# Another order of block products, splits and DMA additions in the up projection of a hybrid transformer block

## The chip, the cores and the metric

The kernel runs on one core of a Trainium2 chip. Its engines work side by side and meet through semaphores: TensorE (PE, with its weight loads as PEld), VectorE (DVE), ScalarE (ACT), GpSimd (POOL) and SyncE (SP). SP issues plain DMA loads; POOL issues the DMAs that add what they read onto what lies in the on-chip buffer. The metric is the device time of one execution in microseconds. The time before is the median of three runs.

## The reference

One layer: a hybrid mixer, a cross attention and a convolutional feed-forward part, each followed by a layer norm. All is float32. The change is in the first half of the feed-forward part:

```python
def conv_ffn(x, w_up, conv_w, conv_b, w_down):
    u = causal_dwconv(x @ w_up, conv_w, conv_b)
    gate, val = jnp.split(u, 2, axis=-1)
    return (jax.nn.gelu(gate) * val) @ w_down
```

Here x is 512 tokens by 1024, w_up is 1024 by 5632 (gate and val have 2816 columns each), and w_down is 2816 by 1024.

## The kernel before

The kernel is one long program of stages; a scheduler places the instructions of each engine in a fixed order when the program is built. Each float32 product is made of three matmuls over a high and a low part: ACT casts the weights to the high part `wh` (line 125), DVE subtracts it to get the low part `wl` (line 126), and PE runs the three matmuls of lines 155 to 157. Four buffers each of `wh` and `wl` rotate, so the cast for a product can start when the product four places earlier is done.

The up projection is cut into 11 quads, q = 0 to 10. A quad takes 256 gate and 256 val columns of w_up, in four blocks B11, B12, B21 and B22 of 128 partitions by 1024 floats (512 KB; the first index is the half of the contraction, the second gate or val). Seven block products M1 to M7 instead of eight make a quad, in the manner of Strassen and Winograd. Each is 24 matmuls of 256 columns. On the side of the tokens the combinations are made once (`forms`, tiles `xf`). On the side of the weights they are made for each quad by DMA, in place:

- M1, M2 and M3 use B11, B21 and B22 as loaded.
- After M3's split, B12 is added onto B22. M7 uses that sum.
- After M1's split, the new B22 is added onto B11. M6 uses that sum.
- After M2's split, the new B11 is added onto B21. M4 uses that sum.
- M5 uses T1, a second copy of B11 onto which B12 is added.

So three additions follow one another, B22, then B11, then B21; this is the chain of weight sums. For q = 0 the sum of B22 is made in a slot of its own (T3) before the stage. The blocks lie in nine slots: halves of the three `raw` buffers, `rawx`, and the two halves of `hf[5]`. In the trace they show as `raw`, `rawx` and `hf`; an addition onto B11 in `raw` from B22 in `hf` is `raw<-hf`, and one that reads B12 from HBM is `raw<-in_ffn_w_up_dram`. A slot is given back when its last product has been split, and `take` hands out the slot that was given back longest ago. Loads stand in order in SP's queue and additions in POOL's; a waiting one holds up what stands behind it.

`seq` (lines 850 to 857) is the order of the products. From q = 3 on a group of seven is M1, M2, M7, M6 of q, M3 of q + 1, then M4, M5 of q. `step(i)` writes product i and, with it, the split of product i + 3, the additions which that split allows, and loads ahead of need (`AHEAD`, lines 994 to 1000). M1, M6 and M5 accumulate in one PSUM bank and M7 and M4 in another: between two of them ACT copies the bank out (`keep`, line 926), so M6 waits for the copy m1, M4 for m7 and M5 for u2. These copies, the splits and the convolution (lines 939 to 946) share ACT and DVE. In the shown rows of engine order `wh_...<-raw_...` is the split of a product, and `m1_`, `m3_`, `m7_`, `u2_` are the copies after M1, M3, M7 and M6.

Of the kernel before, what the change touches and what calls it, by code (L numbers as in the profile page):

```python
# [32 lines left out]
NQ = NPAIR // 2  # L33
# [7 lines left out]
def hybrid_block_kernel(  # L41
# [34 lines left out]
    def mm_bank():  # L76
        return pm.tile([P, 512], F32, name="mm", tag="mm", bufs=5)

    def mx_bank():
        return pm.tile([P, 512], F32, name="mx", tag="mx", bufs=3)  # L80
# [38 lines left out]
    def split(src, shape, skew=0):  # L119
        h = wp.tile([P, 1152], F32R, name="wh", tag="wh", bufs=4)[:, skew:skew + 1024]  # L120
        l = wp.tile([P, 1152], F32R, name="wl", tag="wl", bufs=4)[:, skew:skew + 1024]
        a, c = shape
        hv = h.rearrange("p (a c) -> p a c", a=a)
        lv = l.rearrange("p (a c) -> p a c", a=a)
        A.copy(hv, src)  # L125
        V.tensor_sub(lv, src, f32(hv))  # L126
        return hv, lv
# [141 lines left out]
    def tt(name):  # L269
        return q1p.tile([P, 512], F32, name=name, tag="T", bufs=20)  # L270
# [122 lines left out]
    for i, h, l in col_units(w_in0, HQ, 4):  # L393
        ps = mm_bank()
        col_tile(ps, h, l, feat(xTh), feat(xTl))
        q = tt("q")
# [438 lines left out]
    slots, free = [], list(range(9))  # L835

    def ffn_begin():
# [3 lines left out]
        for q in range(3):  # L841
# [5 lines left out]
    load, add = nc.sync.dma_start, lambda d, s_: nc.gpsimd.dma_start(d, s_, accum_op=OP.add)  # L847
    blk = lambda q, n: ffn_w_up[q, int(n[1]) - 1, int(n[2]) - 1]
    FORM = {"M1": "A11", "M2": "A12", "M3": "S4", "M4": "A22", "M5": "S1", "M6": "S2", "M7": "S3"}
    seq = [(n, q) for q in range(3) for n in ("M1", "M2")]  # L850
    seq += [(n, int(q)) for n, q in (w.split(".") for w in
            "M3.0 M7.0 M6.0 M3.1 M4.0 M5.0 M3.2 M7.1 M6.1 M3.3 M4.1 M5.1 M7.2 M6.2 M4.2 M5.2".split())]
    for q in range(3, NQ):
        if q + 1 < NQ:
            seq += [("M1", q), ("M2", q), ("M7", q), ("M6", q), ("M3", q + 1), ("M4", q), ("M5", q)]
        else:
            seq += [(n, q) for n in ("M1", "M7", "M2", "M6", "M4", "M5")]
    held, units = {}, {}

    def take(q, n):  # L860

        ok = [f for f in free if not (q >= NQ - 2 and 5 <= f < 7) and not (q >= 7 and f == 8)]
        held[q, n] = ok[0]
        free.remove(ok[0])
        return slots[ok[0]]

    at = lambda q, n: slots[held[q, n]]

    def drop(q, n):
        free.append(held.pop((q, n)))  # L870

    def loads(q, names):
        for n in names:
            load(take(q, n), blk(q, n if n != "T1" else "B11"))

    def first_t(q):
        loads(q, ["T1"])
        add(at(q, "T1"), blk(q, "B12"))

    def split_of(i):  # L880

        n, q = seq[i]
        src = {"M1": "B11", "M2": "B21", "M3": "B22", "M4": "B21", "M5": "T1", "M6": "B11", "M7": "B22"}[n]
        if n == "M7" and (q, "T3") in held:
            src = "T3"
        units[i] = split(at(q, src), (8, P), 16)
        t3 = "T3" if (q, "T3") in held else "B22"
        if n == "M1":
            if (q, t3) in held and (q, "summed") in units:
                add(at(q, "B11"), at(q, t3))  # L890
        if n == "M2":
            if (q, "summed") in units:
                add(at(q, "B21"), at(q, "B11"))
        if n == "M3":
            units[q, "summed"] = True
            if t3 == "B22":
                add(at(q, "B22"), blk(q, "B12"))
            else:
                drop(q, "B22")
            if q not in (1, 2):  # L900
                first_t(q)
            if q < 3:
                add(at(q, "B11"), at(q, t3))
                add(at(q, "B21"), at(q, "B11"))
        if n == "M7":
            drop(q, src)
        if n == "M6":
            drop(q, "B11")
        if n == "M5":
            drop(q, "T1")  # L910
        if n == "M4":
            drop(q, "B21")

    def product(bank, i, first, last):
        (h, l), (fh, fl) = units.pop(i), forms[FORM[seq[i][0]]]
        for j in range(2):
            for k in range(4):
                mm3(bank[:, j * 256:(j + 1) * 256], h[:, 4 * j + k, :], l[:, 4 * j + k, :], fh[:, k, :], fl[:, k, :],
                    first and j == 0 and k == 0, last and j == 1 and k == 3)
# [4 lines left out]
    def keep(q, name, bank):  # L924
        t = t2(name)
        A.copy(t, bank)  # L926
        kept[q, name] = g2(t)

    def put(q, c, half, bank, name):
        V.tensor_tensor(uus[q][:, c, :, half * 256:(half + 1) * 256], g2(bank), kept[q, name], op=OP.add)  # L930

    def conv_pieces(q):
        y = {}

        def taps(c, j):
            ft = j * NPAIR + 2 * q + c
            u, f = uus[q][:, c, j, :], t2("fc")
            w = lambda i: ncols[:, i * 44 + ft:i * 44 + ft + 1] if c else col(FCW + i * 44 + ft)
            A.activation(f, u, AF.Identity, bias=col(FCB + ft), scale=w(2))  # L939
            if j:  # L940
                A.activation(y[c, 0], y[c, 0], AF.Gelu_apprx_tanh)  # L941
            for d in (1, 2):
                V.scalar_tensor_tensor(f[:, d:], u[:, :S - d], w(2 - d), f[:, d:], op0=OP.mult, op1=OP.add)  # L943
            y[c, j] = f

        mul = lambda c: V.tensor_mul(hslice(2 * q + c), y[c, 0], y[c, 1])
        return [lambda: taps(1, 0), lambda: taps(1, 1), lambda: (mul(1), taps(0, 0)), lambda: taps(0, 1),
                lambda: mul(0)]

    def step(i):  # L950

        n, q = seq[i]
        if n == "M1":
            banks[q, "P"] = mm_bank()
            uus[q] = (hf[3 + q] if q < 2 else raws[q % 2]).rearrange("p (c j t) -> p c j t", c=2, j=2)
        if n == "M7":
            banks[q, "Q"] = mm_bank()
        if n in ("M2", "M3"):
            banks[q, n] = mx_bank()
        b = banks[q, {"M1": "P", "M6": "P", "M5": "P", "M7": "Q", "M4": "Q"}.get(n, n)]  # L960
        for f in posts:
            f()
        posts.clear()
        if i + 3 < len(seq):
            split_of(i + 3)
        elif i + 3 - len(seq) < len(down_first):
            down_first[i + 3 - len(seq)]()

        for m, names in AHEAD.get(i, ()):
            if names == "T1":  # L970
                first_t(m)
            else:
                loads(m, names)
        product(b, i, n in ("M1", "M2", "M3", "M7"), n in ("M2", "M3", "M4", "M5"))
        if pieces:
            pieces.pop(0)()
        if n == "M1":
            posts.append(lambda: keep(q, "m1", b))
        if n == "M2":
            posts.append(lambda: put(q, 0, 0, b, "m1"))  # L980
        if n == "M3":
            posts.append(lambda: keep(q, "m3", b))
        if n == "M7":
            posts.append(lambda: keep(q, "m7", b))
        if n == "M6":
            posts.append(lambda: keep(q, "u2", b))
        if n == "M5":
            posts.append(lambda: (put(q, 1, 0, b, "m3"), put(q, 1, 1, b, "m7"), pieces.extend(conv_pieces(q))))
        if n == "M4":
            posts.append(lambda: put(q, 0, 1, b, "u2"))  # L990


    where = {w: i for i, w in enumerate(seq)}
    AHEAD = {}
    for q in range(1, NQ):
        if q > 2:
            AHEAD.setdefault(max(where["M3", q] - 8, 1), []).append((q, ["B22"]))
            AHEAD.setdefault(where["M1", q] - 7, []).append((q, ["B11", "B21"]))
    for i, w in ((3, (1, ["B22"])), (6, (2, ["B22"])), (7, (1, "T1")), (12, (2, "T1"))):
        AHEAD.setdefault(i, []).append(w)  # L1000

    hTh, hTl = [], []
# [32 lines left out]
    def ln2_evict(b, ps):  # L1035
        if b == NB - 1:
            for i in range(3):
                split_of(i)
        resid(b, ps, 512, 1024)
        norm(b)  # L1040
        return (lambda: forms_block(b)) if b < 2 else None

    slab(tok(oTh), tok(oTl), ca_wo[0], 512, KT, ln2_evict, late=4, mid=ffn_begin)
    step(0)
    forms_block(2)()
    step(1)
# [29 lines left out]
def build(shapes):  # L1076
    import concourse.bacc as _bacc

    nc = _bacc.Bacc("TRN2", target_bir_lowering=False, num_devices=1, dynamic_dma_scratch_size=1024)
    args = [nc.dram_tensor(f"in_{n}_dram", shapes[n], F32, kind="ExternalInput").ap() for n in _INS]  # L1080
    args.append(nc.dram_tensor("out_0_dram", (1, S, D), F32, kind="ExternalOutput").ap())
    with tile.TileContext(nc) as tc:
        hybrid_block_kernel(tc, *args)
    return nc
# [22 lines left out]
```

## Time and profile before

| | |
|---|---|
| time, median of 3 runs | 827.46 us (824.11 to 829.41) |
| the profiled execution | 824.63 us |
| its span, first to last instruction | 822.9 us |
| mean granted TensorE clock | 0.982 |
| the up projection in it | from about 445 to 695 us of the span |

The profiled execution is near the fastest of the three runs; 1.7 us of it lie outside the span. Stages are told below by microseconds from the span's start.

### The profile page before, as it was taken

The page shows a single profiled execution, that of the slowest core. Times are in us where ns is not written, and L with a number is a line of the kernel's source. Part 1 is how long each engine was busy: PE and PEld are TensorE (multiplying, and loading weights), DVE is VectorE, ACT ScalarE, POOL GpSimd, SP SyncE. Part 2 cuts the span into 40 slices and gives each one's busy share as a digit, 9 for nine tenths or more (in the row PEclk, how much of TensorE's full clock was granted, in tenths as well). Part 3 has the DMA queues.
Part 4 walks back from the last instruction along what each step waited for, and adds up shares of the span by engine and source line. Part 5 has one row for each costly group of instructions (what it writes and reads, how often), then busy time and mean ns, then how long its engine had stood idle before and what let it go on. Part 6 is the DMA issues. An engine that isn't in the chain of part 4 may idle for free. (4 is left out here: it accounts for less than half of the span.)

```text
span 822.9 us, 11742 instructions
## 1 busy us (share of the span) xinstructions
PE 786.5 (96%) x4696; PEld 692.0 (84%) x4696; DVE 569.0 (69%) x944; ACT 374.2 (45%) x512; POOL 68.4 (8%) x96
## 2 busy tenths in 40 slices
PE   8999999999999999999999897799999997999996
PEld 6878877787799888888988897798999987888885
DVE  6364497899785497358369955977798789924237
ACT  3189643453253134247215535665576567621110
POOL 2000100100200010000002021111111110000001
PEclk9999999999999999999999998899999999999999
DMA  9937742254319205331325399777786884442102
GB/s 270 188 75 186 119 79 52 61 102 145 106 49 388 94 18 205 102 103 52 103 103 121 90 215 240 183 192 184 185 183 173 216 199 120 136 154 76 53 1 103
DMA packets 53328, 111.57 MB, mean 136 GB/s; under 512 B 3861, under 2 KB 21397, under 8 KB 53273
## 3 DMA queue, kind: packets, MB, share of 16 engines
q1 hardware_dynamic: 46352, 85.11, 34.7%
q0 software_dynamic: 6336, 23.07, 15.4%
q10 hardware_dynamic: 584, 2.64, 0.9%
q8 instruction: 37, 0.61, 0.3%
q14 instruction: 19, 0.15, 0.1%
HBM read 97.16 MB, written 2.12 MB: 121 GB/s over the span
## 5 line engine op out<-in xcount | busy, mean ns | idle before, releaser
L126 DVE TENSOR_TENSOR wl<-raw,wh 128x1024 fp32r<-128x1024 f32 x143 | 173.9, 1220 | 177.5 <-ACT wh L125 176.9
L125 ACT CAST wh<-raw 128x1024 fp32r<-128x1024 f32 x143 | 149.3, 1050 | 263.3 <-PE mm L157 116.4
L155 PE MATMUL mm<-xf,wh 128*128 128x256 f32 x440 | 126.9, 289 | 20.5 <-ACT m L926 18.4
L156 PE MATMUL mm<-xf,wh 128*128 128x256 f32 x440 | 125.4, 285 | 0.7 <-DVE xf L245 0.7
L157 PE MATMUL mm<-xf,wl 128*128 128x256 f32 x440 | 125.0, 284 | 0.0
L155 PEld LDWEIGHTS mm<-xf,wh 128*128 128x128 f32 x440 | 85.9, 195 | 23.4 <-ACT m L926 20.2
L156 PEld LDWEIGHTS mm<-xf,wh 128*128 128x128 f32 x440 | 86.3, 196 | 1.1 <-DVE xf L245 1.1
L157 PEld LDWEIGHTS mm<-xf,wl 128*128 128x128 f32 x440 | 86.1, 196 | 0.3 <-DVE wl L126 0.3
L156 PE MATMUL mm<-wl,hTh 128*128 128x512 f32 (+1 forms) x180 | 65.9, 366 | 0.0
L155 PE MATMUL mm<-wh,hTh 128*128 128x512 f32 (+1 forms) x180 | 65.8, 366 | 0.0
L157 PE MATMUL mm<-wh,hTl 128*128 128x512 f32 (+1 forms) x180 | 65.8, 365 | 0.0
L155 PE MATMUL mm<-wh,xTh 128*128 128x512 f32 x128 | 52.2, 408 | 0.5 <-DVE xTh L283 0.5
L156 PE MATMUL mm<-wl,xTh 128*128 128x512 f32 x128 | 51.9, 406 | 0.6 <-DVE wl L284 0.6
L157 PE MATMUL mm<-wh,xTl 128*128 128x512 f32 x128 | 51.3, 401 | 0.7 <-DVE xTl L285 0.6
L155 PE MATMUL mx<-xf,wh 128*128 128x256 f32 x176 | 49.8, 283 | 1.0 <-DVE xf L245 1.0
L155 PE MATMUL mm<-xTh,wh 128*128 128x512 f32 x128 | 50.4, 394 | 0.0
L157 PE MATMUL mm<-xTh,wl 128*128 128x512 f32 x128 | 50.4, 394 | 0.0
L156 PE MATMUL mm<-xTl,wh 128*128 128x512 f32 x128 | 50.4, 394 | 0.0
L156 PE MATMUL mx<-xf,wh 128*128 128x256 f32 x176 | 49.5, 281 | 0.0
L157 PE MATMUL mx<-xf,wl 128*128 128x256 f32 x176 | 49.4, 281 | 0.0
L425 POOL TENSOR_TENSOR lnrs<-lnrs,neghalf 128x1 f32<-128x1 f32 x12 | 11.2, 932 | 339.3 <-DVE lnrs L424 339.3
L155 PEld LDWEIGHTS mm<-wh,hTh 128*128 128x128 f32 x180 | 34.0, 189 | 5.6
(318 smaller groups left out, 1808.9 us busy)
## 6 DMA issues: line engine op xcount, KB each, us to landing
raw<-in_ffn_w_up_dram SPq DMA_DIRECT2D x30, 512.0 KB, 4.9
raw<-in_w_in_dram SPq DMA_DIRECT2D x14, 1024.0 KB, 9.3
raw<-in_ffn_w_down_dram SPq DMA_DIRECT2D x10, 1024.0 KB, 5.2
raw<-in_ca_wkv_dram SPq DMA_DIRECT2D x8, 1024.0 KB, 5.4
raw<-in_ffn_w_up_dram POOLq DMA_DIRECT2D x13, 512.0 KB, 5.5
raw<-raw POOLq DMA_DIRECT2D x11, 512.0 KB, 5.5
hf<-in_ffn_w_up_dram SPq DMA_DIRECT2D x10, 512.0 KB, 4.6
raw<-in_w_out_dram SPq DMA_DIRECT2D x4, 1024.0 KB, 9.2
```

The lines of the kernel that those rows point to most:

```text
L125: A.copy(hv, src)
L126: V.tensor_sub(lv, src, f32(hv))
L155: T.matmul(ps, ah, bh, start=first, stop=False, skip_group_check=True)
L156: T.matmul(ps, ah, bl, start=False, stop=False, skip_group_check=True)
L157: T.matmul(ps, al, bh, start=False, stop=last, skip_group_check=True)
L425: G.tensor_tensor(out_, out_, neghalf[:, 0:n], op=OP.pow)
```

## The change

The order of the products changes: M3.1 (M3 of quad 1) comes before M7.0 and M6.0, M3.2 before M4.0, and M1.3 before M4.2. From q = 3 on a group is M2, M7 of q, M3 of q + 1, M6 of q, M1 of q + 1, then M4, M5 of q; the last quad is M2, M7, M6, M4, M5. So M3 is eight products ahead of the M6 of its quad instead of six, and M1 six instead of three. The additions onto B11 and B21 are written with the splits of M1 and M2 for all quads but 1 and 2, whose places come from `AHEAD`. B22 of quads 1 and 2 is loaded one step earlier in the table, and `take` no longer leaves out slot 8 from q = 7 on. No instruction's shape or number changes.

```diff
-            "M3.0 M7.0 M6.0 M3.1 M4.0 M5.0 M3.2 M7.1 M6.1 M3.3 M4.1 M5.1 M7.2 M6.2 M4.2 M5.2".split())]
+            "M3.0 M3.1 M7.0 M6.0 M3.2 M4.0 M5.0 M7.1 M6.1 M3.3 M4.1 M5.1 M7.2 M6.2 M1.3 M4.2 M5.2".split())]
     for q in range(3, NQ):
-        if q + 1 < NQ:
-            seq += [("M1", q), ("M2", q), ("M7", q), ("M6", q), ("M3", q + 1), ("M4", q), ("M5", q)]
-        else:
-            seq += [(n, q) for n in ("M1", "M7", "M2", "M6", "M4", "M5")]
+        later = q + 1 < NQ
+        seq += [("M2", q), ("M7", q)] + [("M3", q + 1)] * later + [("M6", q)] + [("M1", q + 1)] * later
+        seq += [("M4", q), ("M5", q)]
...
-        ok = [f for f in free if not (q >= NQ - 2 and 5 <= f < 7) and not (q >= 7 and f == 8)]
+        ok = [f for f in free if not (q >= NQ - 2 and 5 <= f < 7)]
...
-        if n == "M1":
-            if (q, t3) in held and (q, "summed") in units:
-                add(at(q, "B11"), at(q, t3))
-        if n == "M2":
-            if (q, "summed") in units:
-                add(at(q, "B21"), at(q, "B11"))
+
+        if n == "M1" and q not in (1, 2):
+            add(at(q, "B11"), at(q, t3))
+        if n == "M2" and q not in (1, 2):
+            add(at(q, "B21"), at(q, "B11"))
...
-            if q < 3:
-                add(at(q, "B11"), at(q, t3))
-                add(at(q, "B21"), at(q, "B11"))
...
+            elif names == "T2":
+                add(at(m, "B11"), at(m, "B22"))
+            elif names == "T4":
+                add(at(m, "B21"), at(m, "B11"))
...
-            AHEAD.setdefault(max(where["M3", q] - 8, 1), []).append((q, ["B22"]))
+            AHEAD.setdefault(where["M3", q] - (8 if q > 3 else 6), []).append((q, ["B22"]))
             AHEAD.setdefault(where["M1", q] - 7, []).append((q, ["B11", "B21"]))
-    for i, w in ((3, (1, ["B22"])), (6, (2, ["B22"])), (7, (1, "T1")), (12, (2, "T1"))):
+    for i, w in ((2, (1, ["B22"])), (5, (2, ["B22"])), (7, (1, "T1")),
+                 (8, (1, "T2")), (10, (1, "T4")), (11, (2, "T2")), (12, (2, "T1")), (13, (2, "T4"))):
```

On ACT at the start of the stage, before, these rows stand in a row. They are the splits of M7.0 (`wh_3950`) and M6.0 (`wh_3981`), five form pieces and the copy m1 of quad 2, and the split of M3.1 (`wh_4011`):

```order
L125 CAST wh_3950<-raw_3567 128x1024
L125 CAST wh_3981<-raw_3568 128x1024
L244 CAST xf_3535<-xfr_3539 128x4x128
L244 CAST xf_3536<-xfr_3540 128x4x128
L244 CAST xf_3538<-mx_3892 128x4x128
L244 CAST xf_3537<-xfr_3540 128x4x128
L926 COPY m1_3979<-mm_3948 128x512
L244 CAST xf_3534<-xfr_3541 128x4x128
L125 CAST wh_4011<-hf_3542 128x1024
```

Now the same places hold the splits of M3.1 (`wh_3950`), M7.0 (`wh_3982`) and M6.0 (`wh_4013`):

```order
L125 CAST wh_3950<-hf_3542 128x1024
L125 CAST wh_3982<-raw_3567 128x1024
L244 CAST xf_3535<-xfr_3539 128x4x128
L244 CAST xf_3536<-xfr_3540 128x4x128
L244 CAST xf_3538<-mx_3895 128x4x128
L244 CAST xf_3537<-xfr_3540 128x4x128
L920 COPY m1_3980<-mm_3948 128x512
L244 CAST xf_3534<-xfr_3541 128x4x128
L125 CAST wh_4013<-raw_3568 128x1024
```

The split of M3.1 moved from behind the form pieces to the front, and that of M6.0 to the back. On PE the first two matmuls of M7.0 and of M6.0 stand ahead of M3.0 in both programs.

On POOL from the first addition of the stage on, before, the rows are the additions onto B11 of quad 0, T1.0, B21 of quad 0, a step of the layer norm, then onto B22.1, B11.1, T1.1, B22.2, B21.1, T1.3 and B11.2:

```order
L847 DMA raw_3568<-raw_3567 128x1024
L847 DMA hf_3542<-in_ffn_w_up_dram 128x1024
L847 DMA raw_3568<-raw_3568 128x1024
L425 TENSOR_TENSOR lnrs_3765<-lnrs_3765,neghalf_104 128x1
L847 DMA hf_3542<-in_ffn_w_up_dram 128x1024
L847 DMA raw_3569<-hf_3542 128x1024
L847 DMA raw_3568<-in_ffn_w_up_dram 128x1024
L847 DMA raw_3567<-in_ffn_w_up_dram 128x1024
L847 DMA raw_3569<-raw_3569 128x1024
L847 DMA hf_3542<-in_ffn_w_up_dram 128x1024
L847 DMA rawx_3570<-raw_3567 128x1024
```

Now they are B11.0, B21.0, the step of the norm, T1.0 and B22.1 (the row that counts two), B11.1, T1.1, B22.2, B21.1, B11.2, T1.3 and T1.2 (again two), and B21.2:

```order
L847 DMA raw_3568<-raw_3567 128x1024
L847 DMA raw_3568<-raw_3568 128x1024
L425 TENSOR_TENSOR lnrs_3767<-lnrs_3767,neghalf_104 128x1
L847 DMA hf_3542<-in_ffn_w_up_dram 128x1024 x2
L847 DMA raw_3569<-hf_3542 128x1024
L847 DMA raw_3568<-in_ffn_w_up_dram 128x1024
L847 DMA raw_3567<-in_ffn_w_up_dram 128x1024
L847 DMA raw_3569<-raw_3569 128x1024
L847 DMA rawx_3570<-raw_3567 128x1024
L847 DMA hf_3542<-in_ffn_w_up_dram 128x1024 x2
L847 DMA raw_3567<-rawx_3570 128x1024
```

T1.0 moved behind the norm's step, and T1.3 behind the addition onto B11.2. For q = 3 to 6 the addition onto T1 of the next quad likewise moved from ahead of the one onto B11 to behind it; from q = 7 on POOL's order is the same in both.

On ACT in the middle of the stage, before, from the split of M2.4 (`wh_4733`) to that of M4.4 (`wh_4870`), with M7.4 (`wh_4764`), M6.4 (`wh_4795`) and M3.5 (`wh_4832`) between them:

```order
L125 CAST wh_4733<-rawx_3570 128x1024
L926 COPY m3_4731<-mx_4694 128x512
L125 CAST wh_4764<-raw_3568 128x1024
L125 CAST wh_4795<-raw_3567 128x1024
L939 ACTIVATE fc_4825<-xfr_3540,cols_106,ncols_275 128x512
L125 CAST wh_4832<-hf_3542 128x1024
L926 COPY m1_4830<-mm_4792 128x512
L939 ACTIVATE fc_4863<-xfr_3540,cols_106,ncols_275 128x512
L941 ACTIVATE fc_4825<-fc_4825 128x512
L939 ACTIVATE fc_4899<-xfr_3540,cols_106 128x512
L125 CAST wh_4870<-rawx_3570 128x1024
```

Now, again from the split of M2.4 (`wh_4734`) to that of M4.4 (`wh_4903`), with M7.4 (`wh_4768`), M3.5 (`wh_4797`), M6.4 (`wh_4831`) and M1.5 (`wh_4865`) between them:

```order
L125 CAST wh_4734<-rawx_3570 128x1024
L125 CAST wh_4768<-raw_3568 128x1024
L920 COPY m1_4766<-mm_4731 128x512
L125 CAST wh_4797<-hf_3542 128x1024
L125 CAST wh_4831<-raw_3567 128x1024
L933 ACTIVATE fc_4859<-xfr_3540,cols_106,ncols_275 128x512
L933 ACTIVATE fc_4895<-xfr_3540,cols_106,ncols_275 128x512
L125 CAST wh_4865<-raw_3568 128x1024
L935 ACTIVATE fc_4859<-fc_4859 128x512
L125 CAST wh_4903<-rawx_3570 128x1024
```

The split of M3 of the next quad now stands ahead of that of M6, and the split of M1 of the next quad stands between M6's and M4's. PE's order of whole products follows `seq` from M3.0 on in both programs, but for the two pairs of matmuls told above.

## Rows read from the trace of the kernel before

**Rows 1.** The page, part 1: busy time, share of the span, instructions.
```profile
PE 786.5 (96%) x4696; PEld 692.0 (84%) x4696; DVE 569.0 (69%) x944; ACT 374.2 (45%) x512; POOL 68.4 (8%) x96
```

**Rows 2.** Matmuls that begin and end the stretch: start us, us, engine, line, operation.
```profile
472.18 0.28 PE L157 MATMUL mm<-xf,wl 128*128 128x256 f32 x1
...
694.98 0.40 PE L155 MATMUL mm<-wh,hTh 128*128 128x512 f32 x1
```

**Rows 3.** Windows: length, PE, PEld, DVE, ACT, POOL busy (instructions), clock, DMA share, GB/s.
```profile
472.18:526.82 54.64, 45.33 (x359) 44.94 (x358) 33.92 (x40) 29.29 (x38) 10.41 (x12) 0.88 0.92 224
526.82:695.14 168.32, 157.17 (x1323) 154.66 (x1322) 138.01 (x170) 106.24 (x141) 24.27 (x28) 0.98 0.74 179
526.82:545.86 19.04, 19.04 (x171) 19.04 (x170) 18.35 (x24) 13.11 (x18) 3.49 (x4) 1.00 0.70 176
...
500.00:520.00 20.00, 14.32 (x98) 14.12 (x99) 13.44 (x17) 11.07 (x16) 0.89 (x2) 0.76 0.88 239
```

**Rows 4.** PE's waits from 472.18 to 695.14: us, times, longest.
```profile
PE mm L155 <- ACT m L926: 18.4, 8, 5.1
PE mm L155 <- ACT u L926: 2.1, 5, 0.6
```

**Rows 5.** ACT's longest waits for additions, same stretch.
```profile
ACT wh L125 <- DMA raw<-hf: 27.5, 5, 8.0
ACT wh L125 <- DMA raw<-raw: 22.2, 7, 6.8
...
ACT wh L125 <- DMA raw<-rawx: 7.4, 1, 7.4
...
ACT wh L125 <- DMA rawx<-raw: 5.8, 2, 4.6
```

**Rows 6.** ACT's timeline: splits of M4.2, M6.5 and M4.10.
```profile
513.66 1.05 ACT L125 CAST wh<-raw 128x1024 fp32r<-128x1024 f32 x1 [7.38 <-DMA raw<-rawx]
...
573.53 1.05 ACT L125 CAST wh<-raw 128x1024 fp32r<-128x1024 f32 x1 [7.98 <-DMA raw<-hf]
...
683.14 1.04 ACT L125 CAST wh<-hf 128x1024 fp32r<-128x1024 f32 x1 [2.94 <-DMA hf<-rawx]
```

**Rows 7.** PE's timeline: the first matmuls of M4.2 and M6.5.
```profile
519.48 0.58 PE L155 MATMUL mm<-xf,wh 128*128 128x256 f32 x1 [5.14 <-ACT m L926]
...
576.76 0.39 PE L155 MATMUL mm<-xf,wh 128*128 128x256 f32 x1 [2.37 <-ACT m L926]
```

**Rows 8.** POOL's timeline: additions onto B22.1, B11.1, B21.2, T1.6, B11.5, B21.5.
```profile
473.17 0.89 POOL L847 DMA_DIRECT2D hf<-in_ffn_w_up_dram  x1 [20.26 <-DMA raw<-in_ffn_w_up_dram]
481.41 0.86 POOL L847 DMA_DIRECT2D raw<-hf  x1 [7.35 <-DMA hf<-in_ffn_w_up_dram]
...
502.24 0.86 POOL L847 DMA_DIRECT2D raw<-rawx  x1 [2.21 <-DMA rawx<-raw]
...
565.82 0.88 POOL L847 DMA_DIRECT2D rawx<-in_ffn_w_up_dram  x1 [8.55 <-DMA rawx<-in_ffn_w_up_dram]
566.47 1.12 POOL L847 DMA_DIRECT2D raw<-hf  x1
574.17 0.85 POOL L847 DMA_DIRECT2D raw<-raw  x1 [6.58 <-DMA raw<-hf]
```

**Rows 9.** All additions (line 847), from issue to landing.
```profile
DMA to landing us min/median/max: 4.5/6.2/11.3
```

**Rows 10.** DVE's timeline: the low parts of M7.0 and M6.0.
```profile
468.73 2.35 DVE L126 TENSOR_TENSOR wl<-raw,wh 128x1024 fp32r<-128x1024 f32 x2
```

**Rows 11.** DMA from 526.8 to 695: queues (packets, MB, share of 16 engines), and loads.
```profile
q0 software_dynamic: 4067, 14.76, 48.5%
q1 hardware_dynamic: 4896, 15.21, 25.3%
...
raw<-in_ffn_w_up_dram SPq DMA_DIRECT2D x16, 512.0 KB, 4.8
```

**Rows 12.** DMA from 480 to 520: loads, KB each, median us to landing.
```profile
raw<-in_ffn_w_up_dram SPq DMA_DIRECT2D x5, 512.0 KB, 9.0
```

More of the change, by code (lines that the diff above doesn't have):

```diff
@@ L887, in split_of @@
         t3 = "T3" if (q, "T3") in held else "B22"
-        if n == "M1":
-            if (q, t3) in held and (q, "summed") in units:
-                add(at(q, "B11"), at(q, t3))
-        if n == "M2":
-            if (q, "summed") in units:
-                add(at(q, "B21"), at(q, "B11"))
+        if n == "M1" and q not in (1, 2):
+            add(at(q, "B11"), at(q, t3))
+        if n == "M2" and q not in (1, 2):
+            add(at(q, "B21"), at(q, "B11"))
         if n == "M3":
-            units[q, "summed"] = True
             if t3 == "B22":
```

## The prediction

> **What bounds the kernel now.** I read the page's busy times first. PE is busy 96% of the span [rows 1], so all that can be won lies in its idle and slowed stretches. The windows say where: nearly all of it is in the up projection. From 472.18, when M3.0 is done, to 694.98, when the down projection's first matmul starts, 222.8 us pass [rows 2]. In that stretch stand 70 products of 24 matmuls, less the four matmuls of M7.0 and M6.0 that ran earlier: 1676 matmuls. The reader's yardstick is the window 526.82 to 545.86: one whole group of seven products in 19.04 us, PE busy all the time, clock 1.00 [rows 3]. That is 2.72 us for a product and 0.1133 us for a matmul, so 1676 of them need 189.9 us. The stretch loses 222.8 - 189.9 = 32.9 us. Of that, 54.6 - 40.4 = 14.3 us is lost up to 526.82 (15 products less four matmuls), and 168.2 - 149.6 = 18.6 us on the 55 products behind it.
>
> PE's waits tell what ends 20.5 us of it: always one of ACT's bank copies [rows 4]. The copies themselves are short; ACT comes to them late, since it stands in order and waits in a split for an addition to land. Six kinds of waits for additions on ACT make 70 us in 17 places; the four longest kinds are shown [rows 5]. The other 12.4 us are matmuls at a lower clock behind such a wait, as in 500 to 520 [rows 3], where PE had waited and the granted clock is 0.76, a mean of its two levels 1.2 and 2.4 GHz, and pauses too short for the list.
>
> One chain as a sample, quad 5: the addition onto T1.6 is issued at 565.82, after a wait of 8.55 us for its load; the one onto B11.5 stands behind it and goes at 566.47 [rows 8]; ACT's split of M6.5 has waited 7.98 us when it starts at 573.53 [rows 6]; PE starts M6.5 at 576.76 after 2.37 us [rows 7]. The addition onto B21.5 is issued at 574.17 [rows 8].
>
> **The change, part by part.** The counts of instructions stay, so nothing is saved in work; only waits can go.
>
> *Lead of the chain, q = 4 to 9.* A split runs at best three products ahead of its product, one after the product four places earlier, so I count from split to split. From M3's split the chain needs: split 1.05 us [rows 6] and low part some 1.2 [rows 10], 2.3 in all; addition onto B22 6.2 us (the median [rows 9]); issue 0.6; onto B11 7.1 (566.47 to 573.53); issue 0.6; onto B21 5.5 (574.17 to the next split's start). M6's split is reached after 16.2 us, M4's after 22.3. Before, M6 is 6 products behind M3 (16.3 us) and M4 8 (21.8 us): nothing to spare, and T1's addition, which stood in between, costs more where its load is late. Now they are 8 (21.8 us) and 10 (27.2 us): 5.6 and 4.9 us to spare. The longest PE wait in this part is 2.4 us. Also, M3's split of the next quad no longer stands behind M6's on ACT, so a late landing isn't handed on to the next chain. All 18.6 us can go; I keep 2 us for leftover short pauses, as the five u copies cost 2.1 us in all [rows 4], and 1 us for the last quad, where the lead grows by one product only (2.7 us), while M4.10's split waited 2.94 us [rows 6]. Bounds: 0 and 7 us kept.
>
> *Front, quads 1 and 2.* M3.1's low part takes the place of M7.0's on DVE and ends at 469.9 [rows 10], two low parts and a bank's sum earlier; so B22.1's addition goes out at 470.0 instead of 473.17 [rows 8]. With 8.2 us (473.17 to 481.41) it lands at 478, B11.1 5 us later at 483 (4.5 is the shortest [rows 9]). In this crowded time additions land about every 3.6 us: nine that were issued from 481.41 on have landed by 513.66 [rows 6, 8]. The order is B11.1, T1.1, B22.2, B21.1, B11.2, T1.3, T1.2, B21.2, since T1.3 moved behind: B21.1 lands at 493.8 and B21.2 at 508.2 instead of 513.66. If nothing waits, M4.1 starts 24.0 us after 472.18, at 496.2, and M4.2 at 509.8. From the start of a late split to PE's start it was 3.2 us at M6.5 and 5.8 at M4.2 [rows 6, 7]; ACT's order now has two splits, one step of the convolution and one copy there, like M6.5's, so I take 3.4: the landings are due at 492.8 and 506.4. So M4.1 is 1.0 late and M4.2 another 0.8: 2 us kept of 14.3. With 3.0 us a landing it is 0, with 4.2 about 7.
>
> *Start.* Two matmuls of M6.0 stand ahead of M3.0 on PE, and the split of M6.0 now comes behind the form pieces. PE waits for those pieces anyway until the matmul that follows them; I add 0.5 us, bounds 0 and 2. B22.1's load no longer needs the slot of B22.0, T1.0's now does; T1.0's reader, M5.0, starts near 485, five products behind 472.18, so that costs nothing. On POOL the norm's step stands behind the addition onto B21.0 in both orders.
>
> *Slots.* Blocks are held longer, and two slots are left free at a load instead of three to five. A load still goes out about as soon as the split that frees its slot is done, six products ahead of its use, over 16 us for the 4.8 us that one takes [rows 11]. Nothing. If loads took the 9.0 us of the crowded time [rows 12], still nothing.
>
> *Sum.* 32.9 - 2 - 1 - 2 - 0.5 = 27.4 us. Without them the later stages move up as they are. The profiled execution takes 824.63 us, so 797.2. It is 2.8 us under the median of its runs; taking half of that as chance, I say **799 us**. With the bounds above, 0 to 16 us kept, the case reaches from 793 to 809 on that scale.
>
> The Trainium skill, page "DMA: Bandwidth & Descriptors", section "Anatomy of one DMA — SWDGE (gpsimd) path", gives a DMA issued by GpSimd 2.0 us plus its bytes at 436 GB/s. An estimate from that page is 3.2 us for 512 KB; by it the chain would have fitted before, and the change would bring nothing. The trace disagrees: no addition took under 4.5 us [rows 9].
>
> **The rivals.**
>
> *The DMA engines become the bound.* In 526.8 to 695 28 additions take 48.5% of 168.2 us of the 16 engines, 2.9 us each, and loads 25.3%, 1.47 us for 512 KB [rows 11]. Four of each make 17.5 us of a group's 19.04: 92%. Three loads of 1 MB for the down projection come on top, 1.1 us a group. For: with the waits gone the queue has no rest; additions that start earlier only lengthen each other. Against: the share was 0.92 over the whole front [rows 3]. If only 0.88 can be kept, as in 500 to 520 [rows 3], a group takes 18.6/0.88 = 21.1 us, 2.1 us more in each of eight groups; 17 of the 18.6 us stay, 13.4 us of the whole are won (11.8 in the front and at the start), and the time is 813. The Trainium skill, page "DMA: Bandwidth & Descriptors", section "Issuing engines are not separate DMA queues", says that DMAs from SP and POOL run on the same 16 engines and interleave; this rival is what that would do here.
>
> *It does nothing much.* POOL's order from q = 7 on is the old one; if the additions wait for loads and slots and not for splits, they go out when they did, and the splits wait as long. For: the wait of 8.55 us for T1.6's load [rows 8]. Against: B11.5's addition needs only M1's split and B22, both earlier now. Time 825 to 827.
>
> *Slower: a loop through T1.* The addition onto T1 of the next quad stands ahead of that onto B21 on POOL. Its load waits for a slot that the split of M4 of the quad before gives back; and M4's split waits for B21. Round the loop: load 4.8, issue 0.9, addition 5.5, split and low part 2.3: 13.5 us for a group's 19.04. It decides when load and addition together pass 15.8 us. With 9.0 [rows 12] and 11.3 [rows 9] the loop takes 23.5: 4.5 us over in each of eight groups, 36 us, where 18.6 were lost before. With the front's 12 won that is 830 us or a little more. For: both durations stand in the trace. Against: only in the crowded front, and more late work there makes the queue shorter.
>
> *Another engine.* DVE is busy 18.35 of 19.04 us at PE's full speed [rows 3]. PE lost nothing in that window, so I give it no case of its own, but it is a reason for the kept microseconds.
>
> **How the numbers follow.** The forecast has 74 in 100, the DMA bound 14, nothing much 8, the loop 4. Within 1% (8 us), a measurement of this kernel can hardly tell a change from none. The forecast and the DMA bound at 813 are faster by more than that, but for a tail of the latter: faster 0.87, same 0.09, slower 0.04. The range, 791 to 814, takes in the forecast with its bounds, 2 us of scatter below, and the DMA bound's value.
>
> **What would show it.** The stretch from M3.0's end to the down projection near 195 us; PE's waits for m copies there under 4 us instead of 18.4; ACT's waits for additions under 20 us instead of 70; the clock at 1.00 from 490 on; M4.1 and M4.2 near 497 and 511. A DMA share above 0.95 with waits for additions that stay, on the other hand, would be the DMA bound. Wrong would be: PE waits at M6 or M4 in every group, or a new wait for DVE's low parts, lines 126 and 157, where now there is none.

## The result, and the profile after

The changed kernel takes 804.75 us (median of three runs, 804.43 to 804.93) where the kernel before took 827.46. The ratio is 0.973, with a 95% interval of 0.968 to 0.978: faster. Run once more in six runs beside eleven of the kernel before, it took 801.11 us (796.43 to 802.75) against 825.23, ratio 0.970 (0.966 to 0.973). The forecast was 799, its range 791 to 814.

The profiled execution takes 804.75 us, its span is 803.0. Page, part 1, answers to [rows 1]. PE's busy time falls by 4 us only, and its share rises by a point, since what is won was mostly idle:

```profile
PE 782.3 (97%) x4696; PEld 690.1 (86%) x4696; DVE 569.6 (71%) x944; ACT 375.5 (47%) x512; POOL 68.1 (8%) x96
```

PE's timeline, as [rows 2] and [rows 7]: first matmuls of M3.1 (the stretch begins), M4.1, M4.2 and the down projection:

```profile
472.36 0.28 PE L155 MATMUL mx<-xf,wh 128*128 128x256 f32 x1
...
500.96 0.39 PE L155 MATMUL mm<-xf,wh 128*128 128x256 f32 x1 [1.78 <-ACT m L920]
...
516.70 0.28 PE L155 MATMUL mm<-xf,wh 128*128 128x256 f32 x1
...
675.00 0.40 PE L155 MATMUL mm<-wh,hTh 128*128 128x512 f32 x1
```

The stretch is 675.00 - 472.36 = 202.6 us instead of 222.8. It begins 0.2 us later than before, and what follows it takes the same time, so these 20.2 us, less the 0.2, are the whole of what the profiled execution won (824.63 to 804.75, 19.9 us).

PE's waits in this stretch, as [rows 4]. The m copies have fallen from 18.4 us to 1.8, the u copies are gone, and nothing waits behind 501. Two short waits are new, both at M3.2 near 481, for the high and the low part of its weights:

```profile
PE mm L155 <- ACT m L920: 1.8, 1, 1.8
PE mx L157 <- DVE wl L126: 0.8, 1, 0.8
PE mx L155 <- ACT wh L125: 0.4, 1, 0.4
```

ACT's waits for DMAs in it, all of them, as [rows 5]. They were 70 us for additions; now they are 15, and 10 for loads:

```profile
ACT wh L125 <- DMA raw<-raw: 10.0, 5, 4.4
ACT wh L125 <- DMA raw<-in_ffn_w_up_dram: 9.6, 2, 5.7
ACT wh L125 <- DMA raw<-rawx: 3.3, 1, 3.3
ACT wh L125 <- DMA rawx<-raw: 1.9, 1, 1.9
```

The windows, with the columns of [rows 3]. The first is the front: again 15 products less four matmuls, 356 of them (M1.3 is now among them, and M5.2 no longer). The second is the rest, 55 products or 1320 matmuls, and the third is the old yardstick's 19.04 us:

```profile
472.36:519.53 47.17, 44.23 (x359) 43.62 (x357) 31.50 (x37) 27.09 (x36) 9.34 (x11) 0.96 1.00 251
519.53:675.00 155.47, 155.47 (x1323) 155.47 (x1322) 144.47 (x177) 110.99 (x143) 24.98 (x29) 1.00 0.87 203
526.82:545.86 19.04, 19.04 (x164) 19.04 (x163) 18.66 (x24) 13.48 (x18) 3.90 (x5) 1.00 0.95 211
```

The reader is to see three things. The front takes 47.2 us instead of 54.6, and 40.3 at the yardstick: 6.8 are still lost. Behind it PE is busy in every microsecond at clock 1.00, and still the 1320 matmuls take 155.5 us and not 149.6. And the third line says why: in 19.04 us of full work and full clock there are 164 matmuls where [rows 3] had 171. The matmuls stand 155.47/1320 = 0.1178 us apart, not 0.1133; these two are called the wide and the close spacing below. That is a loss of 5.9 us with no wait in it, and no list of waits shows it.

### The profile page after: what moved, and what is told of

The parts are those of the page before. It is cut to its first block, busy times and chain, and to the rows that moved or that the text cites. A ratio compares the mean times of both kernels' runs of the same rounds, so it can differ in the third digit from the quotient of the medians.

```text
span 803.0 us, 11749 instructions
## 1 busy us (share of the span) xinstructions
PE 782.3 (97%) x4696; PEld 690.1 (86%) x4696; DVE 569.6 (71%) x944; ACT 375.5 (47%) x512; POOL 68.1 (8%) x96
## 4 chain that ended last, share of the span: by engine, by line
PE 80%; DVE 9%; DMA 7%; issue 2%; ACT 1%; POOL 1%; DVEq 0%; SPq 0%; ACTq 0%; POOLq 0%
PE mm L155 23%; PE mm L156 23%; PE mm L157 22%; DMA raw<-in_w_in_dram 4%; PE mx L155 2%; PE mx L156 2%; PE mx L157 2%; DMA raw<-raw 2%; DVE wl L126 1%; PE mx L576 1%; DMA hf<-in_ffn_w_up_dram 1%; PE mx L588 1%; DVE xf L245 1%; PE mx L466 1%; POOL ss L425 1%
## 5 line engine op out<-in xcount | busy, mean ns | idle before, releaser
L126 DVE TENSOR_TENSOR wl<-raw,wh 128x1024 fp32r<-128x1024 f32 x141 | 171.8, 1223 | 161.0 <-ACT wh L125 160.3
L125 ACT CAST wh<-raw 128x1024 fp32r<-128x1024 f32 x141 | 147.6, 1049 | 243.1 <-PE mm L157 122.8
L155 PE MATMUL mm<-xf,wh 128*128 128x256 f32 x440 | 124.6, 283 | 2.9 <-ACT m L920 1.8
L156 PE MATMUL mm<-xf,wh 128*128 128x256 f32 x440 | 124.4, 283 | 0.6 <-DVE xf L245 0.6
L155 PEld LDWEIGHTS mm<-xf,wh 128*128 128x128 f32 x440 | 84.9, 193 | 3.4 <-ACT m L920 2.0
L156 PEld LDWEIGHTS mm<-xf,wh 128*128 128x128 f32 x440 | 83.4, 190 | 0.8 <-DVE xf L245 0.8
L157 PEld LDWEIGHTS mm<-xf,wl 128*128 128x128 f32 x440 | 83.5, 190 | 0.3 <-DVE wl L126 0.3
L157 PEld LDWEIGHTS mm<-wh,hTl 128*128 128x128 f32 x180 | 33.9, 188 | 5.6
```

Of the source, the lines that this page charges most:

```text
L155: T.matmul(ps, ah, bh, start=first, stop=False, skip_group_check=True)
L156: T.matmul(ps, ah, bl, start=False, stop=False, skip_group_check=True)
L157: T.matmul(ps, al, bh, start=False, stop=last, skip_group_check=True)
```

## The experiments

**Each half of the change alone.** Rear only: the old order for quads 0 to 2, with their loads and additions where they were, and the new groups from q = 3.

```diff
-"M3.0 M3.1 M7.0 M6.0 M3.2 M4.0 M5.0 M7.1 M6.1 M3.3 M4.1 M5.1 M7.2 M6.2 M1.3 M4.2 M5.2"
+"M3.0 M7.0 M6.0 M3.1 M4.0 M5.0 M3.2 M7.1 M6.1 M3.3 M4.1 M5.1 M7.2 M6.2 M4.2 M5.2 M1.3"
...
```

> Only the groups from quad 3 on are changed; the order of quads 0 to 2 and their additions stay as before. Theory (the lead of the chain removes the steady waits): the 14.3 us of the front stay lost, the steady waits and the tail's go, 16 to 18 us; the matmuls may run at 118 ns a matmul instead of 113 for part of the stage, which costs up to 6 us. Time 809 to 815, PE waits for m copies only ahead of 530 us. Rival (the gain comes from the front, which sets all that follows): above 820, with PE waits for m copies at M6 and M4 behind 530 us.

Measured 808.77 us (806.75 to 812.92) against 825.91, ratio 0.980 (0.975 to 0.985). Its windows, front and rest:

```profile
470.00:527.80 57.80, 45.86 (x358) 45.12 (x357) 35.37 (x42) 29.23 (x38) 10.40 (x12) 0.91 0.90 217
527.80:683.27 155.47, 155.47 (x1322) 155.47 (x1321) 141.98 (x172) 109.91 (x141) 24.14 (x28) 1.00 0.83 196
```

The front is no better than before, the rest has no wait and the very 155.47 us of the changed kernel. The new groups alone remove the steady waits. They change more than the lead: the addition onto T1 also stands in another place on POOL for q = 3 to 6, and slots are taken otherwise. From q = 7 on POOL's order is the old one, and there too PE had waited in the kernel before (610 to 695.14) and no longer waits:

```profile
PE mm L155 <- ACT m L926: 5.3, 3, 3.5
```

So T1's new place is not needed for that part; for q = 3 to 6 no run parts it from the lead.

Front only: the new order of quads 0 to 2 but with M1.3 behind M5.2, and the old groups.

```diff
-            "... M7.2 M6.2 M1.3 M4.2 M5.2".split())]
+            "... M7.2 M6.2 M4.2 M5.2".split())]
...
-        seq += [("M2", q), ("M7", q)] + [("M3", q + 1)] * later + [("M6", q)] + [("M1", q + 1)] * later
-        seq += [("M4", q), ("M5", q)]
+        if later:
+            seq += [("M1", q), ("M2", q), ("M7", q), ("M6", q), ("M3", q + 1), ("M4", q), ("M5", q)]
+        else:
+            seq += [(n, q) for n in ("M1", "M7", "M2", "M6", "M4", "M5")]
```

> Only the order of quads 0 to 2, their additions and the lead of M3.1 and M3.2 are changed; the groups from quad 3 on are as before. Theory: the front wins 10 to 12 us and the steady waits stay, some 11 to 19 us: time 814 to 818, PE waits for m copies at M6 and M4 of later quads. Rival (the front is what made the later waits): below 808 and no later waits.

Measured 827.57 us (825.89 to 829.87) against 825.91, ratio 1.002 (1.000 to 1.004): nothing is won, which neither theory had. Windows, and PE's first matmuls of M4.2 and M4.10:

```profile
471.98:524.84 52.86, 44.73 (x359) 43.94 (x357) 34.48 (x42) 28.64 (x37) 10.33 (x12) 0.94 0.99 242
524.84:696.14 171.30, 157.31 (x1322) 154.05 (x1321) 138.46 (x170) 106.25 (x140) 24.28 (x28) 0.98 0.74 177
```
```profile
517.64 0.39 PE L155 MATMUL mm<-xf,wh 128*128 128x256 f32 x1 [3.93 <-ACT m L922]
...
688.04 0.58 PE L155 MATMUL mm<-xf,wh 128*128 128x256 f32 x1 [6.25 <-ACT m L922]
```

The front wins 1.8 us here and 7.5 in the changed kernel. M4.2 starts at about the same time in both (517.64 and 516.70); what differs is that M1.3 fills the 3.93 us that PE waits here. The split of M4.2 starts at 513.66 before [rows 6], at 512.16 here, and in the changed kernel at

```profile
512.67 1.05 ACT L125 CAST wh<-raw 128x1024 fp32r<-128x1024 f32 x1 [3.31 <-DMA raw<-rawx]
```

So the sums of the front came hardly earlier; the product put ahead of M4.2 hid their lateness. The rest is 3.0 us longer than before and uses up what the front won: most of it stands at M4.10, where PE waits 6.25 us and 3.55 in the kernel before. Why it waits longer there was not followed up.

**M3's lead without M1's.** M1 of the next quad goes back behind M5.

```diff
-        seq += [("M2", q), ("M7", q)] + [("M3", q + 1)] * later + [("M6", q)] + [("M1", q + 1)] * later
-        seq += [("M4", q), ("M5", q)]
+        seq += [("M2", q), ("M7", q)] + [("M3", q + 1)] * later + [("M6", q)]
+        seq += [("M4", q), ("M5", q)] + [("M1", q + 1)] * later
```

> The changed kernel with M1 of the next quad back behind M5, so that only M3 is early: a group is M2, M7, M3 of q + 1, M6, M4, M5, M1 of q + 1. M3 stands eight products ahead of M6, M1 only four ahead of M6 and five ahead of M4. Theory A (M3 is the head of the chain, its lead is all that counts): 803 to 808, no waits in the groups. Theory B (from M1's split the rest of the chain needs 2.3 + 0.6 + 7.1 + 0.6 + 5.5 = 16 us, M4's split is reached after 13.6): PE waits about 2.4 us at M4 of each quad, 818 to 825.

Measured 816.75 us (814.80 to 817.40) against 826.17, ratio 0.989 (0.987 to 0.991). PE's waits behind the front (518.89 to 686.65), and the longest of them, M4.3:

```profile
PE mm L155 <- ACT m L920: 6.2, 3, 4.5
PE mm L155 <- ACT u L920: 4.9, 3, 2.6
```
```profile
537.19 0.58 PE L155 MATMUL mm<-xf,wh 128*128 128x256 f32 x1 [4.54 <-ACT m L920]
```

Theory A falls: 12 to 16 us of the gain need M1 ahead too. B has the time nearly right (1 us under its range) but not the places; the waits gather at M4.3 and in the last three quads, while the quads between lose a few tenths each.

**No additions.** The kernel before without its additions onto weight blocks: it leaves out the sums, and with them their DMA work.

```diff
-lambda d, s_: nc.gpsimd.dma_start(d, s_, accum_op=OP.add)
+lambda d, s_: None
```

> The kernel before with all additions onto weight blocks left out (M4 to M7 then multiply blocks that are not summed, so the output is not the reference's). Theory (the additions are what the waits for m copies go back to): no PE waits for copies in the whole stretch, front included; 1676 matmuls at 0.113 to 0.118 us make it 190 to 198 us long, time 793 to 803. Rival (ACT's own load or the banks make M6 and M4 late): the waits for m copies stay, time above 815.

Measured 800.74 us in one run. Windows, front and rest:

```profile
473.75:515.68 41.93, 41.93 (x358) 41.93 (x357) 35.50 (x42) 29.66 (x38) 0.00 (x0) 1.00 0.47 151
515.68:671.15 155.47, 155.47 (x1323) 155.47 (x1321) 141.24 (x172) 108.43 (x140) 0.00 (x0) 1.00 0.30 99
```

Every wait of PE in the stretch is gone, in the old order: the additions are what the m copies went back to. And the rest again takes 155.47 us, here with the DMA engines 0.30 busy. So the 0.1178 us are not made by the additions nor by DMA load. This run does not part the chain of additions from the load that they put on the DMA engines; the next one bears on that, in the changed kernel.

**Is DMA the bound?** The changed kernel with the load onto T1 issued twice.

```diff
         loads(q, ["T1"])
+        load(at(q, "T1"), blk(q, "B11"))
```

> The changed kernel with every load onto T1 issued twice into the same slot (the second writes the same values): one more load of 512 KB a quad, 11 in all. Theory (the DMA engines are not the bound, the chain has slack): 804 to 808, no or short waits in the groups. Rival (DMA at its bound): 1.5 us more a quad, 815 or more, with waits for additions and copies in every group.

Measured 821.89 us in one run. By its time alone that is the rival. But the trace says otherwise; a window of the middle, the wait at M4.10, and POOL's rows ahead of that:

```profile
529.00:661.00 132.00, 132.00 (x1167) 132.00 (x1166) 118.66 (x146) 87.73 (x115) 20.88 (x24) 1.00 0.92 227
```
```profile
684.13 0.58 PE L155 MATMUL mm<-xf,wh 128*128 128x256 f32 x1 [9.83 <-ACT m L921]
```
```profile
661.05 0.88 POOL L847 DMA_DIRECT2D rawx<-in_ffn_w_up_dram  x1 [9.50 <-DMA rawx<-in_ffn_w_up_dram]
661.70 1.11 POOL L847 DMA_DIRECT2D hf<-raw  x1
```

In 132 us, nearly seven quads, PE does not wait once, at 0.1133 us a matmul, with a fifth load in each quad. The loss lies in two places: the front (56.3 us instead of 47.2, its DMA share 0.98) and the last quad. There POOL waits for the doubled load of T1.10, and the addition onto B11.10, which stands behind it, goes 0.65 us after T1.10's; the one onto B21.10 follows, and M4.10's split waits 5.78 us for that, until 677.71. So the steady part has room for 1.5 us more of DMA in a quad; what has none is the crowded front, and an addition that stands on POOL behind a late T1.

**One link more in the chain.** The addition onto B21 made twice from q = 3 on, in the changed kernel and in the one before.

```diff
             add(at(q, "B21"), at(q, "B11"))
+            if q > 2:
+                add(at(q, "B21"), at(q, "B11"))
```

> The changed kernel with the addition onto B21 made twice for quads 3 to 10 (M4 multiplies a wrong sum). It makes the chain one link longer, 5.5 to 8 us. Theory (M4 has 4.9 us to spare by the count of products, more by the trace): 0 to 3 us lost in each of eight groups, time 804 to 820. Rival (no slack): 5.5 us or more in each, 845 or more.

> The kernel before with the addition onto B21 made twice for quads 3 to 10 (M4 multiplies a wrong sum). Theory (its chain has nothing to spare): 4 to 6 us lost in each of eight groups, 855 to 875. Rival (the lead is not what the change gives): the same loss as in the changed kernel with the same doubling.

Measured 840.86 us in one run, which is 36 to 40 us over the changed kernel and between the ranges of its theory and its rival, and 862.18, 36 over the kernel before's 825.91. The same loss in both, as the rival said; but POOL's rows of the first show that the experiment did something else than lengthen a chain. The second additions onto B21.4 and B21.5, each with the addition onto B22 of the next quad behind it:

```profile
558.13 0.87 POOL L847 DMA_DIRECT2D rawx<-raw  x1 [9.85 <-DMA rawx<-raw]
558.77 1.12 POOL L847 DMA_DIRECT2D hf<-in_ffn_w_up_dram  x1
...
581.81 0.87 POOL L847 DMA_DIRECT2D raw<-raw  x1 [8.10 <-DMA raw<-raw]
582.46 1.09 POOL L847 DMA_DIRECT2D hf<-in_ffn_w_up_dram  x1
```

The second addition waits on POOL for the first one, and the next quad's chain waits behind it. The additions of one quad then follow those of the quad before, 582.46 - 558.77 = 23.7 us a quad: POOL's order closes a loop, and it takes longer than the 19.04 us that PE needs for a quad. So the equal loss does not show that the lead gives nothing.

The rounds show that it still gives something. From the addition onto B22.5 to the one onto B22.10, five rounds, the changed kernel takes 114.4 us (22.9 each) and the kernel before 129.0 (25.8 each). The addition onto B11.7 in the kernel before:

```profile
630.32 0.85 POOL L847 DMA_DIRECT2D hf<-raw  x1 [11.90 <-DVE wl L126]
```

In the old order the split of M1.7 stands on ACT behind that of M4.6, which at 622.63 has waited 6.47 us for the second addition onto B21.6; so the addition onto B11.7 waits 11.90 us, for the low part of M1.7. In the new order M1.7 is split ahead of M4.6, and the addition goes at 614.32 after 6.67 us, with that low part long made (602.47).

The changed kernel's own loop, without the doubling, additions onto B21.5 and B22.6:

```profile
560.32 0.85 POOL L847 DMA_DIRECT2D raw<-raw  x1 [2.14 <-DVE hf L940]
562.88 0.86 POOL L847 DMA_DIRECT2D hf<-in_ffn_w_up_dram  x1 [1.72 <-DVE wl L126]
```

Here the addition onto B22.6 waits 1.72 us for its own split's low part, so POOL has about that much to spare in this quad; the additions onto B22.5 to B22.10 wait 0.5 to 3.8 us.

**The spacing of the matmuls.** Four transposes into a bank that is overwritten break the stream, ahead of M2.3 alone or ahead of M2 of each quad from 3 on.

```diff
+        if n == "M2" and q == 3:          # second kernel: q >= 3
+            for _ in range(4):
+                T.transpose(b[:, 0:P], ident, ident)
         product(b, i, ...
```

> The changed kernel with four dummy 128x128 transposes into the PSUM bank ahead of M2.3, which is overwritten; no value changes. They break the stream of matmuls once, at about 520 us. Theory (the spacing of 256-column matmuls has two modes, 113 and 118 ns, kept until the stream is broken): behind them matmuls stand 113 ns apart, or the draw is made anew; at 113 to the end the time is 798 to 800. Rival (118 ns is what the stage's DMA or DVE load makes of the matmuls): 118 ns behind them as well, time 805.

> The changed kernel with four dummy 128x128 transposes into the bank ahead of M2 of every quad from 3 on, eight sets in all; no value changes. Theory of two modes: matmuls 113 ns apart in all or nearly all groups; 6 to 7 us won, some 0.6 us paid for each set: 800 to 803. Rival (the load on DMA or DVE makes 118 ns): 118 ns in the groups, time 808 to 811.

Measured 799.53 us (796.25 to 804.82), ratio 0.969 (0.963 to 0.974), and 803.23 (803.07 to 804.50), 0.973 (0.969 to 0.977). PE's timeline of the first shows a slip of 0.39 us from one matmul to the next, and the windows before and behind it:

```profile
558.79 0.28 PE L157 MATMUL mm<-xf,wl 128*128 128x256 f32 x1
559.18 0.39 PE L155 MATMUL mm<-xf,wh 128*128 128x256 f32 x1
```
```profile
523.00:539.00 16.00, 16.00 (x144) 16.00 (x142) 15.96 (x22) 10.56 (x15) 2.58 (x3) 1.00 0.90 202
...
560.00:580.00 20.00, 20.00 (x172) 20.00 (x171) 18.68 (x24) 14.38 (x20) 3.45 (x5) 1.00 0.95 225
```

Behind the transposes 144 matmuls stand in 16 us, the close spacing; behind the slip 172 in 20 us, the wide one, to the end of the stage. This profiled run took 804.82 us, the other three of the same program 796.25 to 801.19. In the second kernel the windows between two sets show the close spacing in seven of eight quads and the wide one in one:

```profile
543.00:561.00 18.00, 18.00 (x155) 18.00 (x155) 17.10 (x22) 12.43 (x17) 3.85 (x5) 1.00 0.96 232
563.00:581.00 18.00, 18.00 (x161) 18.00 (x161) 16.74 (x21) 12.39 (x17) 2.71 (x4) 1.00 0.97 234
```

The two quads have the same work and nearly the same DMA share (0.96, 0.97) and DVE load (17.1, 16.7 us), so the rival falls: load does not make the spacing. What the sets win they cost again.

**The changed kernel again**, with no edit.

> The changed kernel itself, run more often. From about 506 us to the down projection nothing breaks its stream of matmuls. Theory (the spacing is drawn at the last break and kept): times fall in two clusters, near 805 with 118 ns to the end and near 798 to 799 with 113, hardly any between. Rival (this order of instructions always ends in 118 ns): 804 to 806 in all runs.

Measured 801.11 us, as told above: 796.43, then 800.92 to 802.75. The rival falls, and the two clusters are not there either. The profiled run (801.0 us): windows, the first matmul of M4.10, and ACT's copy ahead of it:

```profile
470.56:517.53 46.97, 42.83 (x358) 42.23 (x357) 31.16 (x37) 26.97 (x36) 9.44 (x11) 0.96 1.00 251
517.53:671.34 153.81, 150.78 (x1322) 150.59 (x1321) 142.40 (x175) 109.61 (x142) 25.04 (x29) 1.00 0.88 204
```
```profile
665.78 0.38 PE L155 MATMUL mm<-xf,wh 128*128 128x256 f32 x1 [3.02 <-ACT m L920]
```
```profile
665.15 0.58 ACT L920 COPY m<-mm 128x512 f32<-128x512 f32 x1
```

PE is busy for 150.78 us: the close spacing nearly throughout. Then it waits at M4.10, for the copy of m7, which ACT makes at 665.15, behind a split that waited 1.55 us for an addition, two more splits and steps of the convolution. With the wide spacing PE came to M4.10 later and met no wait. So part of what the close spacing wins is given back at the last quad, and times between the clusters can follow.

**The front once more.** M3.2 behind M4.0, M5.1 ahead of M4.1, M5.2 ahead of M4.2; then the same with one transpose ahead of M2 of each quad from 3 on.

```diff
-"M3.0 M3.1 M7.0 M6.0 M3.2 M4.0 M5.0 M7.1 M6.1 M3.3 M4.1 M5.1 M7.2 M6.2 M1.3 M4.2 M5.2"
+"M3.0 M3.1 M7.0 M6.0 M4.0 M3.2 M5.0 M7.1 M6.1 M3.3 M5.1 M4.1 M7.2 M6.2 M1.3 M5.2 M4.2"
```

> The changed kernel with M3.2 behind M4.0, M5.1 ahead of M4.1 and M5.2 ahead of M4.2; the groups from quad 3 on as in the changed kernel. Theory (what the front still loses are waits for the load of B22.2 and the addition onto B21.1, each reached one product too early): its 3.4 us of waits and 1.8 us of matmuls at 1.2 GHz go, 799 to 800 with 118 ns behind them, 793 to 795 with 113. Rival (the additions only lengthen each other, the waits move on): 803 to 806.

> As front2, and one dummy 128x128 transpose into the bank ahead of M2 of every quad from 3 on, eight in all; no value changes. Theory (one break of the stream lets the spacing be drawn anew): 113 ns in most groups, some 0.2 us paid for each: 795 to 797. Rival (one transpose is too short a break): 118 ns stays where it was, 800 to 802.

Measured 799.36 us (795.24 to 801.04), ratio 0.968 (0.964 to 0.971), and 801.95 (798.99 to 804.00), 0.971 (0.967 to 0.975). The first kernel's windows and all its waits in the stretch:

```profile
470.53:515.89 45.36, 42.22 (x358) 41.83 (x357) 32.36 (x38) 29.29 (x38) 8.62 (x10) 0.96 1.04 263
515.89:665.49 149.60, 149.60 (x1322) 149.60 (x1321) 140.22 (x172) 108.20 (x140) 25.03 (x29) 1.00 0.87 207
```
```profile
PE mm L155 <- ACT u L920: 2.5, 1, 2.5
PE mm L155 <- ACT m L920: 0.6, 1, 0.6
```

The front wins 1.6 to 1.8 us, not 5: the wait moved from M4.1 to the copy u2 ahead of M5.1, as the rival said. This run (795.24 us) is short because its 1320 matmuls take 149.60 us, the yardstick to the hundredth. In the second kernel five quads had the close spacing and three the wide one, so one transpose is break enough; its time misses the 795 to 797 that the close spacing in most groups was to give. Neither stands apart from the changed kernel's 0.970 to 0.973 beyond the intervals; no version here is shown to beat it.

## Why the prediction was right, and where its sum was off

The direction and the mechanism held. The steady waits were a chain of additions with no lead to spare; with the new groups they are gone (rear only), without the lead of M1 a part of them comes back (M3 alone), and without the additions they are gone in the old order too. That the profiled execution ended at 804.75 where the sum gave 797.2 comes from a yardstick that was too short and from the front:

**The yardstick**, "1676 of them need 189.9 us". It was read in one window of the kernel before, and 0.1133 us is only the closer of two spacings. Behind the front the changed kernel ran at 0.1178: 5.9 us more. When it ran at 0.1133 nearly throughout, the kernel took 801.0. Another window of the kernel before, also full and at clock 1.00, shows the same count of matmuls within one in 19.42 us; from 627.1 on they stand 0.1178 us apart:

```profile
616.05:635.47 19.42, 19.42 (x170) 19.42 (x169) 16.57 (x21) 11.32 (x17) 1.74 (x2) 1.00 0.71 173
```

**Front**, 2 us kept; measured 47.2 - 40.3 = 6.8: 2.9 are idle time of PE, some 1.6 the wide spacing, and most of the rest matmuls at a lower clock behind the wait at M4.1 (0.51 was granted from 503 to 506, nearly all of it 1.2 GHz). M4.1 came at 500.96 and M4.2 at 516.70, not near 497 and 511. Three steps failed. B22.1's addition went out at 472.25, not 470.0: M3.1's low part did not take M7.0's place on DVE but came behind the form pieces, at 470.42 to 471.64, and T1.0's addition, issued at 470.23, stood ahead. The addition onto B21.1 took 12.6 us, against the longest of 11.3 in [rows 9], so "about every 3.6 us" did not hold: it landed at 497.7, not 493.8, and the one onto B21.2 at 512.7, not 508.2. And loads were late, as told under *Slots*. DVE's row of M3.1's low part, POOL's rows (B22.1, B21.1), then ACT's (splits of M3.3 and M4.1):

```profile
470.42 1.22 DVE L126 TENSOR_TENSOR wl<-hf,wh 128x1024 fp32r<-128x1024 f32 x1
```
```profile
472.25 0.86 POOL L847 DMA_DIRECT2D hf<-in_ffn_w_up_dram  x1 [1.11 <-issue]
...
485.14 0.86 POOL L847 DMA_DIRECT2D raw<-raw  x1 [1.71 <-DMA raw<-hf]
```
```profile
492.24 1.05 ACT L125 CAST wh<-raw 128x1024 fp32r<-128x1024 f32 x1 [5.74 <-DMA raw<-in_ffn_w_up_dram]
497.73 1.05 ACT L125 CAST wh<-raw 128x1024 fp32r<-128x1024 f32 x1 [4.44 <-DMA raw<-raw]
```

The step from landing to PE's start was right (3.4 us; here 3.2 from the split's start). *Slots*, "nothing", failed here too: M3.3's split waited 5.74 us for B22.3's load, and M3.2's 3.86 for B22.2's. The second cost PE its two new waits, 0.4 and 0.8 us. The 16 DMA engines are busy 1.00 of the front, and with more loads the front took 9.1 us longer; there, and in no other part, they are at or near their bound. The Trainium skill, page "DMA: Bandwidth & Descriptors", section "Issuing engines are not separate DMA queues", says that DMAs started by SP and by POOL run on the same 16 engines and interleave; this front agrees, with a share of 1.00 and 12.6 us for the addition onto B21.1.

**Steady and last quad**, 2 + 1 us kept; measured 0 in this execution, and 3.0 at M4.10 alone in the run with the close spacing. So the term for the last quad was too small, and the wide spacing hid it. **Start**, 0.5: measured 0.2.

By what was measured, 6.8 + 5.9 + 0.2 = 12.9 us of the 32.9 stayed, which gives 20.0 won; the executions differ by 19.9. The sum kept 5.5. That 12.9 still lies within its bounds of 0 to 16 is in part luck, since 5.9 of it, the spacing, had no term at all.

Of the rivals, the DMA bound fell for the groups: share 0.95 with no wait, where it allowed 0.88, and room for one more load a quad. Its price of 813 was 8 us off, and what the groups lost is no DMA wait. "Nothing much" fell with the waits. The loop through T1 was not met, but loops exist: in order on POOL, additions of one quad hold up those of the next, with 0.5 to 3.8 us to spare in a quad, and where T1's load was made late in the last quad the additions behind it cost 9.8 us. Of the signs, PE's waits for m copies (1.8 us, asked under 4) came true; ACT's waits for additions did (15 us, asked under 20), with 10 for loads beside them. The stretch near 195 us was missed, with 202.6 and, in the run again, 200.8; only another order of the front reached it (194.96). The clock reached 1.00 for good behind 506 and not 490. One sign of being wrong came as well, a new wait for a low part on line 157, but once and for 0.8 us, behind the late load of B22.2.

## What to carry to other kernels

Count a chain's lead from split to split in units of the product that PE runs, and compare it with the sum of landings; where nothing is spare, putting all heads of the chain earlier (M1 as well as M3) removes the waits, and M3 alone won less than half. An in-order queue of DMAs can close a loop from one group to the next: check what stands behind each waiting issue. And read a yardstick of full speed in several windows: count matmuls in a window without waits, before promising the time of a gapless stream.

## What the runs showed of the hardware that was not expected

Streams of 128x256 matmuls with a weight load for each, at granted clock 1.00 and with no wait, ran at one of two spacings: 0.1133 us (149.60 us for 1320) or 0.1178 (155.47 us for 1320, the same in three kernels). A spacing was kept through all 1320 of them in these, and where it changed in the traces, the stream had slipped or broken there, by 0.39 us in one case. It does not follow DMA load (wide at share 0.30, close at 0.97) nor the order of products (the same program ran both). Behind four transposes it was the close one in 7 of 8 quads, behind one transpose in 5 of 8. What decides the spacing behind a break stays open; it moves this kernel's time by up to 0.7%, nearly the 1% within which the prediction saw hardly a change.
